# Attention's probabilities and values kept in plain float32, two heads side by side in TensorE's column halves

## The chip, the cores and the metric

The kernel runs on one core of one Trainium2 chip. The metric is the time of one execution in device microseconds (us); the median of three runs is shown.

## The reference

Two layers of a diffusion backbone over 1024 latent tokens and 256 context tokens of width 1024, all in float32. Each layer mixes tokens by attention, by a gated recurrence and by a Fourier transform, all reading one projection, and then applies a gated feed-forward network with a short convolution. What matters here is the attention: 8 query heads and 2 key/value heads of 64 channels.

```python
def attend(q, k, v):
    s = jnp.einsum('bhgqd,bhkd->bhgqk', q, k).astype(jnp.float32) * (HEAD_DIM ** -0.5)
    p = jax.nn.softmax(s, axis=-1).astype(v.dtype)
    return jnp.einsum('bhgqk,bhkd->bhgqd', p, v)
```

Latent tokens read 1280 keys (context and latent); context tokens read the 256 context keys, and only in the first layer.

## The kernel before

Tokens are cut into ten tiles of 128: two of context, eight of latent tokens. Attention (`attention`) works on **units**: one tile of queries and one pair of heads. Layer 0 has 40 units, 8 of them on context tiles; layer 1 has 32. For a unit, `score` multiplies queries by keys (L566, L567) in segments of at most 512 keys, takes the maximum (L569, L572) and the exponential (L576). `value` then multiplies probabilities by V. TensorE sums over the partition axis, so the probabilities must first be turned with the keys on partitions: a **step** takes two tiles of 128 keys and both heads, four transposes of 128x128 (L602), into one PSUM tile `ps_t` of which there are two. A latent unit has five steps, a context unit one: 64 x 5 + 8 = 328 steps.

The kernel's products of float32 numbers use the type `float32r` with operands split into a high part and the remainder. `ph` is the rounded copy of a step's turned probabilities (a cast on ScalarE, L607), `pl` what is left (a subtraction on VectorE, L608). V is stored as high, low, high (`use_kv`, L458 to L460), so that one product of `pl` with (low, high) and one of `ph` with (high, low), each with all 128 columns of the array and 256 moving columns (two heads side by side), add up the four partial products in the two halves of `ps_o`'s partitions. These are L612 and L614: four matmuls a step. At a unit's end the two halves of `ps_o` are added (`oa`, L619; `ob`, L620) and stored (L621). There is one `ps_o`.

`value` of one unit and `score` of the next are generators that alternate. Each step they `yield` a cost, and `interleave` lets the other work of the layer (late projections, then Fourier mixing, then the recurrence) run beside them in proportion; `LACE` has the shares. The order on an engine is fixed when the program is built: instructions are numbered in program order, `ahead(x)` subtracts the offset `AHEAD[layer][x]` from the number of those inside and leaves the counter where it was, and each engine takes the lowest number that is ready. Transposes ("pt") are pulled ahead by 50 in layer 0 and 30 in layer 1, score products ("qk") by 50 and 150; the products with V ("pv") and the split ("split") stay at their place. Beside these streams, on TensorE, run the projections (L158 to L160) and the recurrence's products (L773), which use parts of the array 64 rows by 32 or 64 columns; the products of the adaLN part (L246) use four column strips of 32.

Of the kernel before, what the change touches and what calls it, by code (L numbers as in the profile page):

```python
# [11 lines left out]
F32 = mybir.dt.float32  # L12
# [7 lines left out]
P = 128  # L20
# [5 lines left out]
NT = T // P  # L26
# [19 lines left out]
# how the parts of a layer's token mixing are laced, and which of their instructions go ahead of others  # L46
# [16 lines left out]
P_BUFS = {512: 10, 256: 5}  # L63

# [32 lines left out]
def hybrid_backbone_kernel(ctx: ExitStack, tc: tile.TileContext, A: dict, out: bass.AP):  # L97
# [50 lines left out]
    def w_stream(units, ahead=()):  # L148
        # weights split one unit ahead of the products that take them
        ahead = list(ahead) or [w_split(*units[0])]  # L150
        for n in range(len(units)):
            if n + len(ahead) < len(units) and len(ahead) < 2:
                ahead.append(w_split(*units[n + len(ahead)]))
            yield ahead.pop(0)
# [26 lines left out]
    def columns(pp, specs, eng=None):  # L181
        # parameter rows to one column per 128 of them
# [149 lines left out]
    # ================= token mixing: projections =================  # L332
# [15 lines left out]
    class Stages:  # L348
        # each use of a product runs its later stages after one and two further products
# [49 lines left out]
    def project_qkv(l, ww, hT, st, S, bg, tiles):  # L399
# [56 lines left out]
        def use_kv(i, acc):  # L456
            vv = acc[:, 128:256].rearrange("p (h c) -> p h c", h=2)
            nc.scalar.copy(V[:, i, :, 0, :], vv)  # L458
            nc.scalar.copy(V[:, i, :, 2, :], vv)
            nc.vector.tensor_tensor(out=V[:, i, :, 1, :], in0=vv, in1=f32(V[:, i, :, 0, :]), op=ALU.subtract)  # L460
# [75 lines left out]
    # ================= attention =================  # L536
    def attention(l, S, ap, psn, finished):
# [54 lines left out]
        def value(i, pr):  # L592
# [3 lines left out]
            o = psn.tile([P, 256], F32, tag="o", bufs=1, name="ps_o")  # L596
            for s2 in range(nk // 2):
# [5 lines left out]
                ph = ap.tile([P, 2, 256], F32R, tag="ph", bufs=2, name="ph")  # L603
                pl = ap.tile([P, 2, 256], F32R, tag="pl", bufs=2, name="pl")
                tv = t.rearrange("p s h n -> p s (h n)")
                with ahead("split"):
                    nc.scalar.copy(ph, tv)  # L607
                    nc.vector.tensor_tensor(out=pl, in0=tv, in1=f32(ph), op=ALU.subtract)  # L608
                with ahead("pv"):
                    for ss in range(2):  # L610
                        s = 2 * s2 + ss
                        nc.tensor.matmul(o, lhsT=V[:, s, kv, 1:3, :].rearrange("p a c -> p (a c)"), rhs=pl[:, ss, :],  # L612
                                         start=(s == 0), stop=False)
                        nc.tensor.matmul(o, lhsT=V[:, s, kv, 0:2, :].rearrange("p a c -> p (a c)"), rhs=ph[:, ss, :],  # L614
                                         start=False, stop=(s == nk - 1))
                yield 0.88
            oa = ap.tile([HD, 256], F32, tag="oa", bufs=1, name="oa")
            ob = ap.tile([HD, 256], F32, tag="ob", bufs=2, name="ob")
            nc.scalar.copy(oa, o[64:128, :])  # L619
            nc.vector.tensor_tensor(out=ob, in0=o[0:64, :], in1=oa, op=ALU.add)  # L620
            nc.sync.dma_start(  # L621
                out=S["mixA"][pr * P:(pr + 1) * P, i * P:(i + 1) * P].rearrange("(h v) n -> v h n", v=HD),
                in_=ob.rearrange("p (h n) -> p h n", h=2))
# [4 lines left out]
        for n, u in enumerate(units):  # L628
            gens = [value(*u)] + ([score(*units[n + 1])] if n + 1 < len(units) else [])
            lens = [keys(u[0]) // 2, 2]  # L630
# [28 lines left out]
    # ================= Fourier mixing =================  # L659
# [85 lines left out]
    # ================= gated linear recurrence =================  # L745
    def recurrence(l, S, gp2, gp, psum):
# [18 lines left out]
        def scores(keys, size, moving):  # L765
            # keys of each block of `size` tokens against as many queries; heads of the lower and of the
            # upper 64 channels go to different banks
# [36 lines left out]
        def pair_steps(i):  # L804
            # two tiles of tokens, 2 P of them, side by side
# [111 lines left out]
        # a pair of tiles starts when the one before is halfway  # L917
# [55 lines left out]
    # ================= residual update and layer norm =================  # L973
# [13 lines left out]
    def load_resid(pp, src, ga, ba, bufs=4, after=None, engs=None):  # L987
        r = pp.tile([P, D], F32, tag="r", bufs=bufs, name="r")
        if after is not None:
            # keeps the load, and what it sets off, behind the one that writes `after`  # L990
            nc.scalar.copy(r[:, 0:1], after)
# [32 lines left out]
    # ================= output projection =================  # L1024
# [35 lines left out]
    # ================= gated convolutional feed-forward =================  # L1060
# [24 lines left out]
    def ffn_weights(fp, n, nraw):  # L1085
        # every fourth unit in a place of its own: one more than the common ring holds
# [11 lines left out]
    def conv(l, j, part, o, u):  # L1098
        # u has one token more than o on either side
# [22 lines left out]
    # The up-projection of all latent tokens takes seven products of quarters in place of eight  # L1122
    # (Winograd's form of Strassen's identity). A: rows 1 value, 2 gate; columns 1 the lower, 2 the upper
    # channels. B: rows 1 the lower, 2 the upper channels; columns 1 the later, 2 the earlier tokens.
    #   S1 = A21 + A22   S2 = S1 - A11    S3 = A11 - A21   S4 = A12 - S2
    #   T1 = B12 - B11   T2 = B22 - T1    T3 = B22 - B12   T4 = T2 - B21
# [670 lines left out]
```

## Time and profile before

| | |
|---|---|
| median of 3 runs (lowest, highest) | 3447.15 us (3443.57, 3452.46) |
| profiled execution, first to last instruction (span) | 3438.2 us |
| TensorE (PE) busy | 3118.6 us, 91% |
| weight loads (PEld) busy | 2535.5 us, 74% |
| VectorE (DVE) busy | 2545.4 us, 74% |
| ScalarE (ACT) busy | 1547.9 us, 45% |
| GpSimd (POOL) busy | 1412.7 us, 41% |

The profiled execution is known by its span alone; the runs' times also hold what lies around it. Matmuls overlap each other: a matmul's listed duration is longer than the distance at which the next one can start. So the pace of TensorE is read from the starts, and its busy time as the time in which some matmul was under way.

### The profile page before, as it was taken

The page shows a single profiled execution, that of the slowest core. Times are in us where ns is not written, and L with a number is a line of the kernel's source. Part 1 is how long each engine was busy: PE and PEld are TensorE (multiplying, and loading weights), DVE is VectorE, ACT ScalarE, POOL GpSimd, SP SyncE. Part 2 cuts the span into 40 slices and gives each one's busy share as a digit, 9 for nine tenths or more (in the row PEclk, how much of TensorE's full clock was granted, in tenths as well). Part 3 has the DMA queues.
Part 4 walks back from the last instruction along what each step waited for, and adds up shares of the span by engine and source line. Part 5 has one row for each costly group of instructions (what it writes and reads, how often), then busy time and mean ns, then how long its engine had stood idle before and what let it go on. Part 6 is the DMA issues. An engine that isn't in the chain of part 4 may idle for free.

```text
span 3438.2 us, 55946 instructions
## 1 busy us (share of the span) xinstructions
PE 3118.6 (91%) x20897; PEld 2535.5 (74%) x20897; DVE 2545.4 (74%) x4167; ACT 1547.9 (45%) x3105; POOL 1412.7 (41%) x1138
## 2 busy tenths in 40 slices
PE   6999998989899999887899999998988889998885
PEld 4879976778666777666697888876766668776664
DVE  4614568877798887698766755668877798887888
ACT  4325556664443434333365435655642534444332
POOL 3521105422554444443435351115435645454545
PEclk9999999999999999999999999999989999999998
DMA  7643122127754443655675432122045532225643
GB/s 214 205 149 84 54 90 60 34 57 217 223 180 140 129 130 121 210 197 176 208 213 182 130 103 71 46 89 67 18 132 170 185 110 80 80 74 183 224 161 117
DMA packets 451396, 457.07 MB, mean 133 GB/s; under 512 B 31859, under 2 KB 343604, under 8 KB 451126
## 3 DMA queue, kind: packets, MB, share of 16 engines
q1 hardware_dynamic: 440342, 443.85, 40.9%
q0 software_dynamic: 10784, 9.66, 1.2%
q8 instruction: 165, 2.70, 0.3%
q14 instruction: 105, 0.86, 0.1%
HBM read 358.88 MB, written 94.54 MB: 132 GB/s over the span
## 4 chain that ended last, share of the span: by engine, by line
PE 17%; DVE 14%; issue 7%; POOL 6%; DMA 4%; ACT 2%; SPq 0%; POOLq 0%; DVEq 0%; ACTq 0%
POOL wlo L1216 3%; PE ps_t L602 2%; PE pu L159 2%; PE pu L158 2%; PE pu L160 2%; DVE cv L1105 1%; DVE wlo L1337 1%; PE ps_s L566 1%; DMA araw<-act 1%; PE ps_o L612 1%; PE ps_s L567 1%; PE ps_o L614 1%; PE pws L158 1%; PE pws L159 1%; PE pws L160 1%
## 5 line engine op out<-in xcount | busy, mean ns | idle before, releaser
L1216 POOL TENSOR_TENSOR wlo<-S,whi 128x512 fp32r<-128x512 f32 x176 | 282.5, 1615 | 279.3 <-ACT whi L1215 266.1
L1105 DVE SCALAR_TENSOR_TENSOR cv<-U,cw,cv 128x512 f32<-128x512 f32 x352 | 332.9, 994 | 32.5 <-ACT cv L1102 32.4
L158 PE MATMUL pd<-whi,wlo 128*128 128x512 f32 x616 | 251.4, 419 | 72.7 <-DVE wlo L1337 54.0
L569 DVE TENSOR_REDUCE mx<-ps_s 128x1 f32<-128x512 f32 (+1 forms) x400 | 222.2, 588 | 107.8 <-PE ps_s L567 106.5
L145 POOL TENSOR_TENSOR wlo<-raw,whi 128x1024 fp32r<-128x1024 f32 x69 | 167.4, 2429 | 300.6 <-ACT whi L144 300.6
L608 DVE TENSOR_TENSOR pl<-ps_t,ph 128x512 fp32r<-128x512 f32 x328 | 222.8, 685 | 85.2 <-ACT ph L607 83.0
L602 PE MATMUL ps_t<-ident,p 128*128 128x128 f32 x1312 | 261.9, 283 | 13.1 <-DVE pl L608 7.5
L159 PE MATMUL pd<-wlo,whi 128*128 128x512 f32 x616 | 255.6, 415 | 17.6 <-POOL wlo L1337 17.6
L576 ACT ACTIVATE p<-ps_s,mx 128x512 f32<-128x512 f32 (+1 forms) x400 | 242.7, 615 | 51.8 <-DVE mx L572 42.1
L607 ACT CAST ph<-ps_t 128x512 fp32r<-128x512 f32 x328 | 190.8, 589 | 160.8 <-PE ps_o L614 80.6
L160 PE MATMUL pd<-whi 128*128 128x512 f32 x616 | 252.0, 409 | 0.0
L1102 ACT ACTIVATE cv<-U,cb,cw 128x512 f32<-128x512 f32 x176 | 137.2, 812 | 254.3 <-DVE U L1231 209.6
L158 PE MATMUL pxs<-whi,hlo 128*128 128x256 f32 x752 | 221.6, 295 | 5.7 <-DVE hraw L1504 4.3
L1337 POOL TENSOR_TENSOR wlo<-raw,whi 128x1024 fp32r<-128x1024 f32 (+1 forms) x60 | 156.5, 2616 | 160.2 <-ACT whi L1336 151.0
L159 PE MATMUL pxs<-wlo,hhi 128*128 128x256 f32 x752 | 216.5, 288 | 0.5 <-DVE wlo L145 0.4
L160 PE MATMUL pxs<-whi,hhi 128*128 128x256 f32 x752 | 216.4, 288 | 0.0
L158 PEld LDWEIGHTS pd<-whi,wlo 128*128 128x128 f32 x616 | 122.0, 199 | 114.8 <-DVE wlo L1337 56.1
L612 PE MATMUL ps_o<-pl,V 128*128 128x256 f32 x656 | 200.4, 322 | 6.7 <-DVE pl L608 4.8
L1216 POOL TENSOR_TENSOR wlo<-raw,whi 128x512 fp32r<-128x512 f32 x108 | 149.9, 1395 | 128.0 <-ACT whi L1215 119.1
L556 POOL DMA_DIRECT2D qt<-QT x72 | 40.3, 560 | 373.9 <-PE ps_s L567 277.1
L602 PEld LDWEIGHTS ps_t<-ident,p 128*128 128x128 f32 x1312 | 164.2, 143 | 36.5 <-DVE pl L608 12.3
L1231 DVE TENSOR_TENSOR U<-pu,U 128x512 f32<-128x512 f32 x252 | 167.3, 685 | 25.5 <-PE pu L160 17.2
(395 smaller groups left out, 9680.2 us busy)
## 6 DMA issues: line engine op xcount, KB each, us to landing
raw<-in_w_up_dram SPq DMA_DIRECT2D x144, 512.0 KB
raw<-in_w_down_dram SPq DMA_DIRECT2D x102, 512.0 KB
raw<-in_w_ada_dram SPq DMA_DIRECT2D x96, 512.0 KB
araw<-act SPq DMA_DIRECT2D x80, 512.0 KB
act<-cv SPq DMA_DIRECT2D x88, 256.0 KB
raw<-in_w_in_dram SPq DMA_DIRECT2D x36, 512.0 KB
y<-r SPq DMA_DIRECT2D x28, 512.0 KB
r<-y SPq DMA_DIRECT2D x26, 512.0 KB
```

The source lines that it names most:

```text
L158: nc.tensor.matmul(o, lhsT=al, rhs=bh, start=start, stop=False)
L159: nc.tensor.matmul(o, lhsT=ah, rhs=bl, start=False, stop=False)
L160: nc.tensor.matmul(o, lhsT=ah, rhs=bh, start=False, stop=stop)
L569: nc.vector.tensor_reduce(out=mx[:, j:j + 1], in_=t[:, 0:n], axis=AX.X, op=ALU.max)
L576: nc.scalar.activation(out=t, in_=sc[j][:, 0:n], func=AF.Exp, bias=mx[:, 3:4], accum_out=su[:, h, j:j + 1])
L602: nc.tensor.transpose(t[:, ss, h, :], in_=ps2[h][2 * s2 + ss], identity=ident)
L607: nc.scalar.copy(ph, tv)
L608: nc.vector.tensor_tensor(out=pl, in0=tv, in1=f32(ph), op=ALU.subtract)
L612: nc.tensor.matmul(o, lhsT=V[:, s, kv, 1:3, :].rearrange("p a c -> p (a c)"), rhs=pl[:, ss, :], start=(s == 0), stop=False)
L1105: nc.vector.scalar_tensor_tensor(out=o, in0=u[:, tap:tap + n], scalar=convw[l][tap][:, c:c + 1], in1=o, op0=ALU.mult, op1=ALU.add)
L1216: nc.gpsimd.tensor_tensor(out=lo, in0=src, in1=f32(hi), op=ALU.subtract)
L1337: eng.tensor_tensor(out=lo, in0=src, in1=f32(hi), op=ALU.subtract)
```

## The change

The turned probabilities are copied once, in plain float32, to `tt` (eight buffers): steps 1 and 3 by VectorE, the others by ScalarE. V is stored once, in plain float32. The products of a unit are no longer made step by step: after its last step, one burst of 20 calls (4 for a context unit) multiplies V (128 keys by 64 channels) by 128 columns of one head; the first head's result goes to the lower 64 partitions of `ps_o`, the second head's to the upper 64, in turn. `ps_o` has 128 columns in place of 256 and holds finished sums, so `oa` and the addition go; `ob` is a copy. The costs that `value` yields sum to the same for a unit, half of it behind the burst, and its number of pieces in the alternation with `score` is one more. `AHEAD` and `LACE` stay as they are. Comments are removed throughout; the rest of the diff is this:

```diff
+TT_BUFS = 8
+TT_DVE = (1, 3)
...
         def use_kv(i, acc):
             vv = acc[:, 128:256].rearrange("p (h c) -> p h c", h=2)
-            nc.scalar.copy(V[:, i, :, 0, :], vv)
-            nc.scalar.copy(V[:, i, :, 2, :], vv)
-            nc.vector.tensor_tensor(out=V[:, i, :, 1, :], in0=vv, in1=f32(V[:, i, :, 0, :]), op=ALU.subtract)
+            nc.scalar.copy(V[:, i, :, :], vv)
...
-            o = psn.tile([P, 256], F32, tag="o", bufs=1, name="ps_o")
+            turned = []
             for s2 in range(nk // 2):
                 t = psn.tile([P, 2, 2, P], F32, tag="pt", bufs=2, name="ps_t")
                 with ahead("pt"):
                     for ss in range(2):
                         for h in range(2):
                             nc.tensor.transpose(t[:, ss, h, :], in_=ps2[h][2 * s2 + ss], identity=ident)
-                ph = ap.tile([P, 2, 256], F32R, tag="ph", bufs=2, name="ph")
-                pl = ap.tile([P, 2, 256], F32R, tag="pl", bufs=2, name="pl")
-                tv = t.rearrange("p s h n -> p s (h n)")
+                tt = ap.tile([P, 2, 2, P], F32, tag="tt", bufs=TT_BUFS, name="tt")
                 with ahead("split"):
-                    nc.scalar.copy(ph, tv)
-                    nc.vector.tensor_tensor(out=pl, in0=tv, in1=f32(ph), op=ALU.subtract)
-                with ahead("pv"):
-                    for ss in range(2):
-                        s = 2 * s2 + ss
-                        nc.tensor.matmul(o, lhsT=V[:, s, kv, 1:3, :].rearrange("p a c -> p (a c)"), rhs=pl[:, ss, :],
-                                         start=(s == 0), stop=False)
-                        nc.tensor.matmul(o, lhsT=V[:, s, kv, 0:2, :].rearrange("p a c -> p (a c)"), rhs=ph[:, ss, :],
-                                         start=False, stop=(s == nk - 1))
-                yield 0.88
-            oa = ap.tile([HD, 256], F32, tag="oa", bufs=1, name="oa")
-            ob = ap.tile([HD, 256], F32, tag="ob", bufs=2, name="ob")
-            nc.scalar.copy(oa, o[64:128, :])
-            nc.vector.tensor_tensor(out=ob, in0=o[0:64, :], in1=oa, op=ALU.add)
-            nc.sync.dma_start(
-                out=S["mixA"][pr * P:(pr + 1) * P, i * P:(i + 1) * P].rearrange("(h v) n -> v h n", v=HD),
-                in_=ob.rearrange("p (h n) -> p h n", h=2))
+                    if s2 in TT_DVE:
+                        nc.vector.tensor_copy(tt, t)
+                    else:
+                        nc.scalar.copy(tt, t)
+                turned.append(tt)
+                yield 0.44
+
+            o = psn.tile([P, P], F32, tag="o", bufs=1, name="ps_o")
+            with ahead("pv"):
+                for s in range(nk):
+                    for h in range(2):
+                        nc.tensor.matmul(o[64 * h:64 * h + 64, :], lhsT=V[:, s, kv, :], rhs=turned[s // 2][:, s % 2, h, :],
+                                         start=(s == 0), stop=(s == nk - 1))
+            ob = ap.tile([P, P], F32, tag="ob", bufs=2, name="ob")
+            nc.vector.tensor_copy(ob, o)
+            nc.sync.dma_start(out=S["mixA"][pr * P:(pr + 1) * P, i * P:(i + 1) * P], in_=ob)
+            yield 0.44 * (nk // 2)
...
-            lens = [keys(u[0]) // 2, 2]
+            lens = [keys(u[0]) // 2 + 1, 2]
...
-        S["V"] = kvp.tile([P, NT, 2, 3, HD], F32R, name="V")
+        S["V"] = kvp.tile([P, NT, 2, HD], F32, name="V")
```

## Rows read from the trace of the kernel before

**Rows 1.** Four stretches: start:end, length, busy PE, PEld, DVE, ACT, POOL, clock, DMA share, GB/s.
```profile
314.00:478.00 164.00, 161.47 (x1139) 145.52 (x1138) 95.65 (x214) 97.98 (x249) 21.93 (x21) 1.00 0.26 78
520.00:760.00 240.00, 217.55 (x3529) 178.33 (x3527) 193.35 (x478) 162.31 (x446) 101.64 (x136) 0.94 0.16 42
2095.00:2286.00 191.00, 189.40 (x1311) 165.96 (x1310) 126.27 (x264) 126.08 (x324) 23.93 (x24) 1.00 0.23 68
2305.00:2512.00 207.00, 187.25 (x2837) 148.18 (x2837) 168.58 (x395) 128.63 (x347) 89.40 (x117) 0.96 0.14 40
```
**Rows 2.** Groups by line, weight loads: busy, mean ns, idle before and its releasers.
```profile
L602 PEld LDWEIGHTS ps_t<-ident,p 128*128 128x128 f32 x1312 | 164.2, 143 | 36.5 <-DVE pl L608 12.3 <-issue 5.2 <-ACT p L576 3.3
L612 PEld LDWEIGHTS ps_o<-pl,V 128*128 128x128 f32 x656 | 126.4, 193 | 22.9 <-DVE pl L608 9.6 <-DVE ob L620 3.8 <-issue 2.2
L566 PEld LDWEIGHTS ps_s<-KT,qt 128*128 128x128 f32 x400 | 73.5, 192 | 33.5 <-ACT p L576 22.1 <-DMA qt<-QT 3.2
```

**Rows 3.** Groups by line: the split of the turned probabilities and a PSUM copy.
```profile
L608 DVE TENSOR_TENSOR pl<-ps_t,ph 128x512 fp32r<-128x512 f32 x328 | 222.8, 685 | 85.2 <-ACT ph L607 83.0
L607 ACT CAST ph<-ps_t 128x512 fp32r<-128x512 f32 x328 | 190.8, 589 | 160.8 <-PE ps_o L614 80.6 <-PE ps_t L602 71.2 <-DVE mx L572 2.0
L302 DVE COPY stT<-pT 128x512 f32<-128x512 f32 x28 | 19.1, 682 | 4.1 <-PE pT L294 4.1
```

**Rows 4.** Timeline of TensorE, 557.9 to 559.4 us (start, duration, instruction).
```profile
557.98 0.28 PE L612 MATMUL ps_o<-pl,V 128*128 128x256 f32 x1
558.10 0.28 PE L614 MATMUL ps_o<-ph,V 128*128 128x256 f32 x1
558.30 0.85 PE L773 MATMUL psc<-W 64*64 64x64 f32 x32
559.09 0.64 PE L602 MATMUL ps_t<-ident,p 128*128 128x128 f32 x2
```

**Rows 5.** Timeline of TensorE, 484.2 to 487 us: plain float32, 512 columns.
```profile
484.28 2.74 PE L728 MATMUL pq<-st,at 128*128 128x512 f32 x6
486.86 0.38 PE L602 MATMUL ps_t<-ident,p 128*128 128x128 f32 x2
```

**Rows 6.** Timeline of TensorE, 1202.0 to 1203.8 us, and the tile pada (min/median/max).
```profile
1202.16 0.40 PE L159 MATMUL pu<-T3l,whi 128*128 128x512 f32 x1
1202.40 0.39 PE L160 MATMUL pu<-T3h,whi 128*128 128x512 f32 x1
1202.72 0.64 PE L246 MATMUL pada<-raw,scol 128*32 128x256 f32 x8
1203.29 0.51 PE L158 MATMUL pu<-T4h,wlo 128*128 128x512 f32 x1
...
L246 PE MATMUL pada<-raw,scol x768: 379/403/637, 5.6 to 1394.4; 128*32 128x256 f32 x192
```

**Rows 7.** Groups by line, weight loads, 285 to 785 us.
```profile
L773 PEld LDWEIGHTS psc<-W 64*64 64x64 f32 x160 | 5.0, 149 | 3.0 <-issue 1.2 <-POOL W L875 1.0
```

**Rows 8.** Timeline of TensorE, 373.4 to 374.6 us.
```profile
373.51 0.37 PE L612 MATMUL ps_o<-pl,V 128*128 128x256 f32 x1
373.72 0.27 PE L602 MATMUL ps_t<-ident,p 128*128 128x128 f32 x1
373.74 0.36 PE L614 MATMUL ps_o<-ph,V 128*128 128x256 f32 x1
373.94 0.27 PE L602 MATMUL ps_t<-ident,p 128*128 128x128 f32 x1
```

**Rows 9.** Timeline of TensorE, 613.7 to 615.2 us.
```profile
613.77 0.33 PE L602 MATMUL ps_t<-ident,p 128*128 128x128 f32 x1
614.02 0.25 PE L773 MATMUL psc<-W,kc 64*32 64x32 f32 x2
614.20 0.33 PE L602 MATMUL ps_t<-ident,p 128*128 128x128 f32 x1
```

## The prediction

> **What bounds the kernel now.** I read the four stretches in which attention runs beside other work first [rows 1]: layer 0 beside the late projections (314 to 478 us) and beside the recurrence (520 to 760), then the same two of layer 1. Beside the projections TensorE is busy 161.5 of 164 us and 189.4 of 191; beside the recurrence 217.6 of 240 and 187.3 of 207. VectorE is at 58 to 81%, ScalarE at 60 to 68%. So in these 802 us TensorE sets the pace: it has 46 us of visible idle time, nearly all beside the recurrence, and work taken from VectorE and ScalarE is worth only the TensorE idle time that it caused.
>
> Next I read the groups by line for what that idle time waits on [rows 2]. The weight loads of the turning transposes (L602) and of the products (L612) waited 12.3 and 9.6 us for `pl` (the subtraction on VectorE that closes a step's split and frees its `ps_t` buffer), the product another 3.8 us for `ob`, which frees the single `ps_o`; the transposes waited 3.3 us and the score products (L566) 22.1 us for the exponentials on ScalarE. Together 51 us out of some 800: this is all that shorter queues can give back.
>
> **The change, part by part.** There are 72 pairs of heads ("units"): 64 with five steps of two key tiles, 8 with one step; 328 steps.
>
> *VectorE and ScalarE.* VectorE loses 328 subtractions of 0.685 us (223 us) and gains 128 copies (steps 1 and 3 of 64 units) at the 0.682 us of a copy of the same shape out of PSUM: 87 us, net 136 less. ScalarE loses 328 casts of 0.589 us and gains 200 copies of that price, net 75 less [rows 3]. `oa` and two instructions per tile of V go too. On the path to the end this counts only through the waits above: all of `pl` and `ob` (25.7 us) and, since the exponentials queue behind less, about half of the 25.4 us behind them: -38 us. Bounds: -15, if the copies simply take the place of `pl` as the releaser of `ps_t`, and -60, if the recurrence's VectorE steps also come sooner.
>
> *The products alone.* Before, a step's four products of 256 columns follow each other at 0.12 us [rows 4], so the 20 of a unit take 2.40 us. A plain float32 product runs as two passes: six passes of 512 columns take 484.28 to 486.86, 0.43 us each [rows 5], so a pass of 128 columns needs 0.107 us. Forty passes in two column halves are 20 rounds if the halves run together. That they can is in the trace twice: 32 matmuls of 64 columns on 64x64 tiles, 0.054 us each, end within 0.85 us [rows 4], half of what they would need one after another; and eight passes of 256 columns in four column strips, 0.215 us each, end within 0.64 us, where one by one they would need 1.7 [rows 6]. One of the eight lasts 0.38 us at least, so the last starts 0.26 after the first, and the second round of four begins at 0.24, not 0.215: 0.025 over for four tiles in turn. With two I take half of that, 0.12 us a round, 2.40 us a unit: no gain and no loss. Bounds 0.107 and 0.14 us a round: -16 to +26 us over 64 units.
>
> A rule speaks against this. The Trainium skill ("TensorE: Matmul & The Clock Gate", Part 3, The mechanism) says that a weight load overlaps running matmuls only where the row group differs, and column halves share it. The only 64-column load here lasts 0.149 us [rows 7]; with it exposed in each of 20 rounds the burst would be some 3 us longer, about +190 us in all. The trace bears it out poorly: in [rows 6] the four strips share their rows, and both rounds with eight loads still end in 0.64 us.
>
> *Going in and out.* From a full-width product to a tiled one the next start comes after 0.20 instead of 0.12 us [rows 4], and after 0.32 instead of 0.24 [rows 6]: +0.08. On the way out the last pass in [rows 6] starts at 1202.72 + 0.26 and streams for 0.215, to 1203.19; the next product starts at 1203.29: +0.10. Before, a unit's products switch nothing. 72 x 0.18 = +13 us.
>
> *Interruptions.* This is the term that decides. The order on TensorE is fixed when the program is built: every instruction gets the next number in program order, those under `ahead` get that number less an offset and leave the counter alone, and TensorE takes the lowest number that is ready. Where two streams share numbers they alternate one by one; 373.51 to 373.94 shows product, transpose, product, transpose [rows 8]. Today this costs nothing: transpose and product together take 0.23 us, 0.11 + 0.12. In a burst each alternation leaves the column mode and comes back. [Rows 9] price that: with single tiled products between transposes a cycle takes 0.43 us, 0.25 in and 0.18 out. Less the transpose (0.11) and two passes of 32 columns (0.05) that is 0.27, of which 0.03 is the second pass's weight load, hidden in a pass of 0.107. Besides, a call between two transposes has no partner: 0.215 instead of 0.12. So 0.24 + 0.10 = 0.34 us per interruption.
>
> How many? A burst takes 20 numbers, b to b+19; copy and store make 22. Then the other stream runs for 2.2 of the unit's 6.55 cost points. Beside the projections of layer 0 it has about 52 numbers a unit, so 17 follow on average (in lumps of 26), and the next unit's first transposes stand at b+39, less the offset of 50: b-11, ahead of the burst. But its steps 1 to 4 come within some 5 to 30 numbers more (b+3 to b+15, 16 transposes), and its score products, also pulled by 50, near b. They fall into the burst's own numbers; two `ps_t` buffers and eight `tt` buffers hold back only some. I take 6 interruptions a burst for the 15 units beside projections and Fourier. Beside layer 0's recurrence a unit is about 160 numbers long, 40 follow the burst, and the first step lands near b+12, the others beyond: 3 each for 17 units. In layer 1 the transposes are pulled by 30 alone and land at or behind the burst's end; score products are pulled by 150 and come whenever a `ps_s` buffer comes free: 1.2 each for 32 units. 90 + 51 + 38 = 179, x 0.34 = +61 us. Bounds: none (0), and ten in every burst (640 x 0.34 = +218).
>
> *The rest.* The store keeps its number and bytes on SyncE's queue. The loads of q on GpSimd keep their place. The smaller `ps_o` is now held for a burst, not for a whole unit; its wait is counted above. The new wait, of the first product of a burst for the last `tt`, has the burst and nothing else behind it on TensorE; the transposes are pulled 30 to 50 numbers ahead of it, so the copy is done: nothing. A copy that waits for one of the eight `tt` buffers holds up maxima on VectorE or exponentials on ScalarE behind it, but the buffer comes free after the burst's first four products: inside the bounds of the first term.
>
> **Sum:** 0 + 13 + 61 - 38 = +36 us. The profiled execution had 3438.2 us from its first to its last instruction, so 3474; the median run of 3447.15 lies 8.95 above that span, so 3483 for a run.
>
> **Rivals.**
> 1. *The bursts stay whole* (faster). If nothing enters them, the third term goes: 0 + 13 - 38 = -25, 3422; with the better bounds of products and waits 3384. For it: the 51 us of waits are real, and a product of the next unit enters only if its numbers and its buffers fit. Against it: in layer 0 the numbers coincide, and the alternation in [rows 8] is just that. It decides from below about one interruption a burst: 64 x 0.34 = 22 us leaves nothing over the waits.
> 2. *A draw.* A third to half of the interruptions, 25 us, eat what the waits give: 3447.
> 3. *The halves do not run together* (or their loads lie open, as the rule above has it). Forty passes of 0.107 are 4.3 us instead of 2.4: +122 over 64 units; with 13 for the switches, 179 x 0.24 = 43 for interruptions, which then break no pair, and -38: +140, 3587. Against it stand [rows 4] and [rows 6]; for it only that no row here has 128 rows by 64 columns.
> 4. *A large part of the gain is real but in the wrong place.* Beside the projections TensorE has 4 us of idle time in 355 us [rows 1]; if the relief lands there, it is worth nothing, and the first term shrinks to its bound of -15: 3506. This belongs to the forecast's upper side.
>
> **Numbers.** Forecast (with the fourth case) 0.50, its own range 3460 to 3530; whole bursts 0.28; draw 0.14; serial halves 0.08. Leaving out a tenth on either side gives 3412 to 3545. A measurement of this kernel tells about 0.3%, 10 us, from no change: faster by more 0.27, within 0.15, slower 0.58.
>
> **What would show it.** Burst alone: where 40 passes of `ps_o` follow each other, first to last start near 2.3 us; 4.2 would be serial halves. Switches: 0.25 us from a transpose to a product of the burst, about 0.2 back. Interruptions: in layer 0 beside the projections, transposes between single products of `ps_o`, six or so a unit, few in layer 1; so layer 0's attention should grow by more than layer 1's. Waits: none left for `pl` or `ob`, those of L566 for exponentials halved. VectorE should fall by about 150 us and ScalarE by about 100 without a matching fall of the span. I am wrong if bursts are contiguous in layer 0, or if a transpose in a burst costs less than 0.2 us.

## The result, and the profile after

The changed kernel takes 3550.35 us (median of 4 runs, 3545.81 to 3553.13) against 3445.36 us (4 runs) of the kernel before, run beside it: a ratio of 1.0304, with a 95% interval of 1.0289 to 1.0319. That is 105 us more, where 36 had been forecast; the time lies 20 us beyond the forecast's own range (3460 to 3530) and 5 beyond the wide one (3412 to 3545). The profiled span grew from 3438.2 to 3549.6 us.

The page's first part, and the four stretches in which attention runs beside other work (the columns are those of [rows 1]; the stretches are moved to where this kernel does the same work):

```profile
PE 3241.6 (91%) x22209; PEld 2552.6 (72%) x22209; DVE 2436.5 (69%) x3947; ACT 1453.1 (41%) x2885; POOL 1415.0 (40%) x1138
...
320.00:484.00 164.00, 164.00 (x1163) 128.88 (x1161) 55.73 (x125) 66.61 (x175) 19.90 (x17) 1.00 0.16 49
558.00:822.00 264.00, 241.07 (x3868) 176.92 (x3867) 172.61 (x430) 137.90 (x390) 102.86 (x136) 0.95 0.14 40
2160.00:2380.00 220.00, 219.86 (x1622) 169.81 (x1621) 98.79 (x220) 107.07 (x285) 23.75 (x24) 1.00 0.20 59
2405.00:2618.00 213.00, 198.31 (x3097) 145.81 (x3096) 148.20 (x350) 106.81 (x300) 87.80 (x112) 0.94 0.13 38
```

VectorE is busy 109 us less and ScalarE 95 us less than before; TensorE is busy 123 us more, and its idle time (span less busy) went from 320 to 308 us. So the loss is TensorE's own, and of what the two relieved engines gave, these 12 us of idle time are the most that shows. In the stretches beside projections TensorE has no idle time left to see: 164.00 of 164 us and 219.86 of 220, where [rows 1] had 161.47 of 164 and 189.40 of 191.

Where in the program it went is told by the turning transposes, which run from the first to the last unit of a layer. The view is that of one tile (count, least/median/greatest ns, first and last start); first the kernel before, layer 0 and layer 1, then after:

```profile
L602 PE MATMUL ps_t<-ident,p x672: 270/272/477, 289.8 to 756.2; 128*128 128x128 f32 x168
...
L602 PE MATMUL ps_t<-ident,p x640: 270/272/476, 2095.5 to 2519.7; 128*128 128x128 f32 x160
```
```profile
L602 PE MATMUL ps_t<-ident,p x672: 270/273/476, 290.0 to 810.2; 128*128 128x128 f32 x168
...
L602 PE MATMUL ps_t<-ident,p x640: 270/273/476, 2157.3 to 2618.9; 128*128 128x128 f32 x160
```

Layer 0's attention grew from 466.4 to 520.2 us, layer 1's from 424.2 to 461.6: +54 and +37 of the 111 us by which the profiled span grew. The other 20 us lie between and behind these stretches (8 and 12), and no run says what they are; two runs of the kernel before can differ by as much (3433.63 to 3458.81 us in one set of 19).

The groups by line that answer to [rows 2] and [rows 3] (busy, mean ns, then idle before and its releasers; L602 transposes, L616 products, L606 and L608 the copies, L619 the last copy):

```profile
L602 PEld LDWEIGHTS ps_t<-ident,p 128*128 128x128 f32 x1312 | 162.9, 142 | 67.1 <-issue 45.0 <-ACT tt L608 3.4 <-ACT p L576 2.4
L616 PEld LDWEIGHTS ps_o<-tt,V 128*64 128x64 f32 x2624 | 170.4, 138 | 68.4 <-issue 34.5 <-DVE tt L606 2.4 <-DVE ob L619 2.1
L566 PEld LDWEIGHTS ps_s<-KT,qt 128*128 128x128 f32 x400 | 74.7, 195 | 38.0 <-ACT p L576 15.8 <-issue 9.0 <-DMA qt<-QT 3.0
...
L606 DVE COPY tt<-ps_t 128x512 f32<-128x512 f32 x128 | 87.9, 687 | 97.4 <-PE ps_t L602 96.5
L608 ACT COPY tt<-ps_t 128x512 f32<-128x512 f32 x200 | 117.6, 588 | 229.6 <-PE ps_t L602 228.8
L619 DVE COPY ob<-ps_o 128x128 f32<-128x128 f32 x72 | 20.8, 288 | 55.0 <-PE ps_o L616 54.5
```

What the loss looks like stands in the word "issue": weight loads that waited for nothing that the profile shows. It was 5.2 and 2.2 us for these two lines in [rows 2] and is 45.0 and 34.5. The waits for `pl` are gone, as foreseen, and small ones for `tt` stand in their place.

Now the timelines. A whole burst, by itself, and one in layer 0 beside projections (start, duration, instruction; a call is two passes, so x2 is one call and x40 the whole unit):

```profile
2234.83 0.52 PE L567 MATMUL ps_s<-KT,qt 128*128 128x256 f32 x2
2235.28 2.40 PE L616 MATMUL ps_o<-tt,V 128*64 128x128 f32 x40
2237.61 0.33 PE L602 MATMUL ps_t<-ident,p 128*128 128x128 f32 x1
```
```profile
334.65 0.28 PE L162 MATMUL pxs<-whi,hhi 128*128 128x256 f32 x1
334.86 1.31 PE L616 MATMUL ps_o<-tt,V 128*64 128x128 f32 x18
336.09 0.33 PE L602 MATMUL ps_t<-ident,p 128*128 128x128 f32 x1
336.35 0.43 PE L616 MATMUL ps_o<-tt,V 128*64 128x128 f32 x2
336.71 0.33 PE L602 MATMUL ps_t<-ident,p 128*128 128x128 f32 x1
336.97 0.43 PE L616 MATMUL ps_o<-tt,V 128*64 128x128 f32 x2
337.34 0.44 PE L602 MATMUL ps_t<-ident,p 128*128 128x128 f32 x2
```

The first shows the halves running together: 40 passes from the first start to the last end in 2.40 us. The last pass lasts some 0.27, so the first and last starts are 2.13 us apart, 0.11 us a round. The second shows the interruption: from 336.09 to 336.71 one transpose and one call take 0.62 us. Before, a transpose and a product took 0.23 [rows 8]; +0.39 for each. Counted by the order of starts, the products stand on TensorE in 409 runs instead of 72, so they are interrupted 337 times; 308 of the runs hold an odd number of calls, and one call in them has no partner in the other half. Layer 1, for which few interruptions were expected, has 144 of the 337; transposes stand in 114 of these and score products in 34. One of its bursts beside the projections, cut by score products, and a part of another, cut by transposes:

```profile
2180.88 0.65 PE L616 MATMUL ps_o<-tt,V 128*64 128x128 f32 x6
2181.46 0.50 PE L566 MATMUL ps_s<-KT,qt 128*128 128x512 f32 x1
2181.80 0.40 PE L567 MATMUL ps_s<-KT,qt 128*128 128x512 f32 x1
2182.12 1.09 PE L616 MATMUL ps_o<-tt,V 128*64 128x128 f32 x16
2183.15 0.50 PE L566 MATMUL ps_s<-KT,qt 128*128 128x512 f32 x1
...
2184.04 1.30 PE L616 MATMUL ps_o<-tt,V 128*64 128x128 f32 x18
```
```profile
2302.99 0.65 PE L616 MATMUL ps_o<-tt,V 128*64 128x128 f32 x6
2303.57 0.33 PE L602 MATMUL ps_t<-ident,p 128*128 128x128 f32 x1
2303.83 0.43 PE L616 MATMUL ps_o<-tt,V 128*64 128x128 f32 x2
2304.20 0.33 PE L602 MATMUL ps_t<-ident,p 128*128 128x128 f32 x1
```

### The profile page after: what moved, and what is told of

The parts are those of the page before. It is cut to its first block, busy times and chain, and to the rows that moved or that the text cites. A ratio compares the mean times of both kernels' runs of the same rounds, so it can differ in the third digit from the quotient of the medians.

```text
span 3549.6 us, 57914 instructions
## 1 busy us (share of the span) xinstructions
PE 3241.6 (91%) x22209; PEld 2552.6 (72%) x22209; DVE 2436.5 (69%) x3947; ACT 1453.1 (41%) x2885; POOL 1415.0 (40%) x1138
## 5 line engine op out<-in xcount | busy, mean ns | idle before, releaser
L602 PE MATMUL ps_t<-ident,p 128*128 128x128 f32 x1312 | 290.6, 294 | 3.3 <-ACT p L576 1.8
L616 PE MATMUL ps_o<-tt,V 128*64 128x128 f32 x2624 | 271.4, 289 | 3.6 <-DVE tt L606 1.9
L616 PEld LDWEIGHTS ps_o<-tt,V 128*64 128x64 f32 x2624 | 170.4, 138 | 68.4 <-issue 34.5
L608 ACT COPY tt<-ps_t 128x512 f32<-128x512 f32 x200 | 117.6, 588 | 229.6 <-PE ps_t L602 228.8
L602 PEld LDWEIGHTS ps_t<-ident,p 128*128 128x128 f32 x1312 | 162.9, 142 | 67.1 <-issue 45.0
```

Source lines behind the costliest of these rows:

```text
L602: nc.tensor.transpose(t[:, ss, h, :], in_=ps2[h][2 * s2 + ss], identity=ident)
L616: nc.tensor.matmul(o[64 * h:64 * h + 64, :], lhsT=V[:, s, kv, :], rhs=turned[s // 2][:, s % 2, h, :], start=(s == 0), stop=(s == nk - 1))
```

## The experiments

Theory: the order on TensorE cuts the bursts, each cut costs a change of the array's division in and out, and the lighter load of VectorE and ScalarE is worth little. Rivals: the products themselves are slower; the halves run one after the other; the shorter queues are worth tens of microseconds and hide a still larger loss. Ratios are to the kernel before, run on the same chip; brackets hold 95% intervals.

**The bursts whole** (from the changed kernel). The calls are pulled far ahead, and the first call reads the copy made last, so that it waits for all of them and nothing comes between; 72 runs.

```diff
-..."pt": 50, "split": 0, "pv": 0, ...
+..."pt": 50, "split": 0, "pv": 300, ...
-..."pt": 30, "split": 0, "pv": 0, ...
+..."pt": 30, "split": 0, "pv": 300, ...
-                for s in range(nk):
+                for s in range(nk - 1, -1, -1):
...
-                                         start=(s == 0), stop=(s == nk - 1))
+                                         start=(s == nk - 1), stop=(s == 0))
```

> The changed kernel with its bursts kept whole: the products with V get a low number (ahead by 300) and each burst begins with the last step's keys, so that all its 20 calls become ready at once; the program then has 72 unbroken runs on TensorE in place of 409. Theory (each entry into and exit from the column halves costs about 0.29 us, each call left without its partner 0.11 us): 337 runs x 0.29 + 308 x 0.11 = 131 us less than the changed kernel, about 3420. Rival (the products come too late in a unit, or plain float32 passes are slow by themselves): no change, about 3550. Second rival (switches cost it, but the relief of VectorE and ScalarE is worth nothing): about 3455.

3465.16 us, 1.0054 [1.0033, 1.0074]: +19 us. Of the 105 us, 86 go with the 337 interruptions: 0.255 us each, if the whole bursts lose nothing by their own order (the clock, further down, speaks against that). What is left, products, 72 ways in and out and whatever the relief gives, adds up to +19, where the forecast without interruptions had -25. The weight loads of [rows 2] stand idle for as long as before, 41.7 and 16.9 us in place of 36.5 and 22.9; the copies are named where `pl` was:

```profile
L602 PEld LDWEIGHTS ps_t<-ident,p 128*128 128x128 f32 x1312 | 165.1, 145 | 41.7 <-ACT tt L608 8.7 <-issue 7.9 <-DVE tt L606 6.2
L616 PEld LDWEIGHTS ps_o<-tt,V 128*64 128x64 f32 x2624 | 151.5, 144 | 16.9 <-ACT tt L608 11.3 <-issue 1.1 <-ACT kc L835 0.9
```

**Only the relief** (from the kernel before). The low part of the probabilities is left out, and the product that took it takes the rounded copy `ph` once more: no subtraction, no wait for it, the copies divided between VectorE and ScalarE as in the change; the number and shape of the products stay.

```diff
-                pl = ap.tile([P, 2, 256], F32R, tag="pl", bufs=2, name="pl")
...
-                    nc.scalar.copy(ph, tv)
-                    nc.vector.tensor_tensor(out=pl, in0=tv, in1=f32(ph), op=ALU.subtract)
+                    if s2 in (1, 3):
+                        nc.vector.tensor_copy(ph, tv)
+                    else:
+                        nc.scalar.copy(ph, tv)
...
-..., rhs=pl[:, ss, :],
+..., rhs=ph[:, ss, :],
```

> The kernel before with the relief of VectorE and ScalarE alone: the subtraction is left out and the product that took the remainder takes the rounded copy again, so the low part of the probabilities is left out of the result; steps 1 and 3 are copied by VectorE, the others by ScalarE. TensorE's instructions are the same in number and size. Theory: the relief is worth the waits that it removes, 25 to 40 us, about 3410. Rival (TensorE is the bound and the waits only move): 3435 to 3450.

3454.71 us, 1.0019 [1.0003, 1.0035]: nothing gained. The same lines as in [rows 2], of this kernel (L613 is the first product):

```profile
L602 PEld LDWEIGHTS ps_t<-ident,p 128*128 128x128 f32 x1312 | 168.3, 144 | 34.9 <-ACT ph L609 7.7 <-DVE ph L607 6.4 <-ACT p L576 3.7
L613 PEld LDWEIGHTS ps_o<-ph,V 128*128 128x128 f32 x656 | 128.4, 196 | 22.9 <-DVE ph L607 5.8 <-ACT ph L609 3.6 <-DVE ob L621 3.4
```

The waits changed their names: 34.9 and 22.9 us of idle time, as 36.5 and 22.9 before. The copy that replaces the subtraction ends the same idle time.

**Relief and burst, at full width** (the same, with the products of a unit in one burst behind its last step, five `ph` buffers).

```diff
+                turned.append(ph)
+                yield 0.44
...
+            with ahead("pv"):
+                for s in range(nk):
+                    ph = turned[s // 2]
...
```

> As the relief alone (low part of the probabilities left out), and the products of a unit deferred into one burst as in the change, but at the full width of the array in float32r, with five buffers of turned probabilities. Theory (a burst is slow only because it changes the array's mode): within 10 us of the relief alone, whatever runs between its products. Rival (the deferral and the interruptions themselves cost): 80 to 110 us above the relief alone.

3436.68 us, 0.9969 [0.9955, 0.9983]: 11 us faster than the kernel before, 18 faster than the relief alone and some 114 faster than the change, though its products stand in 394 runs, nearly as many as the 409 of the change. So neither the burst nor the number of its cuts costs by itself; the cuts cost where the products divide the array otherwise than their neighbours. That a cut at full width is free altogether is argued from [rows 8], not shown: the kernel before has its products in 500 runs, and no full-width burst was kept whole. This is also the run in which relief shows: the idle time before the same loads (L617 is the first product) fell from 59.4 us together to 40.4.

```profile
L603 PEld LDWEIGHTS ps_t<-ident,p 128*128 128x128 f32 x1312 | 166.4, 143 | 30.8 <-ACT ph L610 6.7 <-DVE ph L608 3.1 <-issue 3.0
L617 PEld LDWEIGHTS ps_o<-ph,V 128*128 128x128 f32 x656 | 127.4, 194 | 9.6 <-DVE ob L624 5.0 <-DVE ph L608 1.5 <-issue 0.3
```

**One full-width float32 call for both heads** (from the changed kernel). V twice side by side, so that one call of 256 columns makes both heads' sums without column halves; half of the results are not used.

```diff
-                    for h in range(2):
-                        nc.tensor.matmul(o[64 * h:64 * h + 64, :], lhsT=V[:, s, kv, :], rhs=turned[s // 2][:, s % 2, h, :],
-                                         start=(s == 0), stop=(s == nk - 1))
+                    nc.tensor.matmul(o, lhsT=V[:, s, kv, :, :].rearrange("p a c -> p (a c)"), rhs=turned[s // 2][:, s % 2, :, :].rearrange("p h n -> p (h n)"),
+                                     start=(s == 0), stop=(s == nk - 1))
```

> The changed kernel with its products at the full width: V is stored twice side by side (128 columns) and one plain float32 matmul takes both heads (256 moving columns), in the same bursts without protection; the program has 286 runs of them on TensorE. Theory: no mode changes, but each pair of key tiles costs two passes of 0.215 us in place of 0.235 together: 656 x 0.195 = 128 us over the kernel before, less 25 to 40 of relief: 3530 to 3545. Rival (an interruption of a plain float32 burst costs whatever its width): 286 x 0.3 more, about 3620.

3550.43 us, 1.0306 [1.0278, 1.0334]: the same time as the change, by another way. Its whole burst:

```profile
2201.83 4.48 PE L616 MATMUL ps_o<-tt,V 128*128 128x256 f32 x20
```

4.48 us instead of 2.40, 133 us over 64 units, and no change of division: since the times are equal, the column halves save some 130 us of product time against this form and lose about as much at their edges. Against the full-width burst above it is 114 us more, not even the whole 133; so its 286 runs leave no price for a cut of plain float32 as such.

**Four calls a step, no burst** (from the changed kernel, calls pulled by 300): 288 whole runs, 248 of four calls and 40 of eight.

```diff
-                turned.append(tt)
-                yield 0.44
+                with ahead("pv"):
+                    for ss in range(2):
+                        s = 2 * s2 + ss
+                        for h in range(2):
+                            nc.tensor.matmul(o[64 * h:64 * h + 64, :], lhsT=V[:, s, kv, :], rhs=tt[:, ss, h, :],
+                                             start=(s == 0), stop=(s == nk - 1))
+                yield 0.88
```

> The changed kernel without the burst: four calls in the column halves right after each step's copy, each group kept whole (ahead by 300); 288 unbroken runs on TensorE, none with an odd number of calls, in place of the 72 of the whole bursts. Theory (a clean entry and exit cost about 0.29 us): 216 x 0.29 = 63 us above the whole bursts, about 3528. Rival (what whole bursts lose comes from their late place in a unit, not from switches): at or below the whole bursts, 3440 to 3465.

3523.56 us, 1.0226 [1.0196, 1.0257]. Against the whole bursts 58.4 us for 216 more runs: 0.27 us for a clean way in and out, with whatever else their other place in the unit is worth. By that price the 72 of the whole bursts cost 19 us, which is all that they lose; products, waits and the granted clock together then come to nothing.

**The heads in turn** (the whole bursts, with all calls of one head before those of the other).

```diff
-                for s in range(nk - 1, -1, -1):
-                    for h in range(2):
+                for h in range(2):
+                    for s in range(nk - 1, -1, -1):
```

> The whole bursts with one loop turned round: all ten calls of the first head, then all ten of the second, instead of the heads in turn. Theory (halves run together only if neighbouring calls go to different halves): a burst takes 40 passes of 0.11 us one after another in place of 20, 64 x 2.2 = 137 us above the whole bursts, about 3602. Rival (the order of calls does not matter to the overlap): 3465.

3568.36 us, 1.0354 [1.0318, 1.0390], 103 us over the whole bursts. One burst:

```profile
2244.01 4.20 PE L616 MATMUL ps_o<-tt,V 128*64 128x128 f32 x40
```

4.20 us instead of 2.40: in one half the passes follow each other at about 0.10, in two halves in turn at 0.11 for two. Only the order of the calls was changed, so it is the alternation that makes the halves overlap.

**Transposes at their own place** (from the changed kernel).

```diff
-..."pt": 50, ...
+..."pt": 0, ...
-..."pt": 30, ...
+..."pt": 0, ...
-                    with ahead("qk" if (i, pr) != units[0] else "pt"):
+                    with ahead("qk"):
```

> The changed kernel with one number altered: the transposes are no longer pulled ahead (offset 0 in place of 50 and 30), so the next unit's transposes keep their place behind the burst; the program has 181 runs of products in place of 409, 108 of them with an odd number of calls in place of 308. Theory (the pulled transposes cut the bursts): with 0.29 us a run and 0.11 us an odd run, 43 us above the whole bursts, about 3508, some 42 us below the changed kernel. Rival (transposes at their place come too late for their copies, and TensorE waits): no gain over the changed kernel, 3550 or more.

3437.50 us, 0.9976 [0.9957, 0.9994]. The expectation was too high by 70 us. 181 runs are left, and 228 fewer at 0.255 are 58 us of the 113 gained. The other 55 may in part be the transposes themselves: they now stand in 279 groups instead of 756, and go over to or come from the recurrence's tiled products 99 times instead of 262. What that is worth no run separates; in the kernel before, the same edit takes 17 us off TensorE's busy time (below).

**Products one step later** (from the kernel before: three buffers each of `ph` and `pl`, nine of the probabilities' long segments instead of ten, the products of a step issued behind the next step's split).

```diff
+                if held:
+                    products(*held)
+                held = (s2, ph, pl)
                 yield 0.88
+            products(*held)
```

> The kernel before with the products of each step put behind the next step's turning (three buffers of each half of the split, nine of the probabilities' long segments), at the full width with the exact split. Theory (part of what the full-width burst gained, 18 us against the relief alone, comes from products that never wait for their split): 5 to 15 us below the kernel before. Rival (it came from the unit's order as a whole, or from fewer interruptions): no change, 3440 to 3455.

3454.87 us, 1.0024 [1.0008, 1.0040]: a miss. The waits were moved rather than taken away. The products (L602 here) wait 2.0 us for `pl` instead of 9.6, but 8.4 for `ob` instead of 3.8, and the transposes (L613 here) stand idle for 36.5 us as before:

```profile
L613 PEld LDWEIGHTS ps_t<-ident,p 128*128 128x128 f32 x1312 | 165.3, 143 | 36.5 <-DVE pl L619 9.6 <-issue 7.6 <-ACT p L576 2.1
L602 PEld LDWEIGHTS ps_o<-pl,V 128*128 128x128 f32 x656 | 126.4, 193 | 18.4 <-DVE ob L628 8.4 <-issue 2.0 <-DVE pl L619 2.0
```

**The offset of the transposes in the kernel before.** The edit of "Transposes at their own place", made in the kernel before.

> The kernel before with one number altered: the transposes are not pulled ahead (offset 0 in place of 50 and 30). It separates what pulled transposes cost other streams from what they cost the bursts. Theory (of the 113 us that this number was worth in the changed kernel, 83 came from the cut bursts and some 28 from transposes that cut the recurrence's tiled products and the projections): 20 to 30 us below the kernel before, about 3420. Rival (in the full-width kernel a transpose between other products costs nothing, and without the pull the products wait for their split): 3445 or more.

3439.76 us, 0.9985 [0.9973, 0.9997]: 5 us. So the 113 us of that edit in the changed kernel belong to it together with the column halves. Here it gives and takes: TensorE was busy for 3101.4 us of its span of 3439.0, 17 us less than before, but idle for 18 more. The products' weight loads (columns as in [rows 2]) now wait for `pl`, 55.0 us instead of 9.6:

```profile
L612 PEld LDWEIGHTS ps_o<-pl,V 128*128 128x128 f32 x656 | 125.4, 191 | 66.7 <-DVE pl L608 55.0 <-DVE mx L572 1.8 <-DVE ob L620 1.4
```

**Whole bursts and transposes at their place** (both edits in the changed kernel).

> The whole bursts (72 runs) and the transposes at their place together. Theory (both remove cuts, and cuts are all that the change costs): the 109 runs and 108 odd runs that the transposes at their place still leave are worth 0.27 and 0.11 us each, so 41 us below that kernel, about 3397. Rival (a burst forced whole loses as much by pushing all other work back, as the whole bursts' 28 us above the full-width burst suggest): 3430 to 3445.

3449.56 us, 1.0008 [0.9995, 1.0021]: no better with 72 runs than the 3437.50 with 181. To force a burst whole seems to have a price. One candidate is the granted clock. Beside the recurrences of the whole-burst kernel (columns as in [rows 1]):

```profile
526.00:796.00 270.00, 236.17 (x3904) 189.65 (x3905) 184.15 (x455) 143.70 (x400) 109.80 (x142) 0.89 0.19 56
2319.00:2545.00 226.00, 199.63 (x3203) 157.86 (x3202) 154.85 (x373) 113.44 (x315) 88.44 (x116) 0.89 0.14 42
```

0.89 is the mean of 2.4 GHz and stretches at 1.2; it was 0.95 and 0.94 in the change and 0.94 and 0.96 in [rows 1]. Summed over the clock's records, TensorE was at 1.2 GHz for 330 us in the whole bursts, 327 in this kernel, 263 with transposes at their place alone and 260 before. What in the order makes it fall was not tried, and that it is the cause of the lost time is argued, not shown. The runs allow an estimate: over the 77 runs of the kernel before, beside which the experiments ran, the time falls by about 2.0 us for each 0.001 of mean granted clock (3456.32 us at 0.957, 3435.35 at 0.964), and the mean of the whole bursts' runs is 0.953 against 0.960. That would be 15 of their 19 us. It would also be the 12 us between this kernel (0.956) and the one with the transposes alone at their place (0.962). No run sets the clock by itself. The change as it was given has 0.960, as the kernel before, so the clock is no part of its 105 us.

**All offsets of attention's matmuls at 0** (from the changed kernel): as "Transposes at their own place", and the score products too.

```diff
-    {"qk": 50, ... "pt": 50, ...
-    {"qk": 150, ... "pt": 30, ...
+    {"qk": 0, ... "pt": 0, ...
+    {"qk": 0, ... "pt": 0, ...
```

> The changed kernel with transposes and score products both at their place (offset 0 for both in both layers): 122 runs of products, 42 of them odd, nothing forced. Theory (cuts alone): 59 x 0.27 + 66 x 0.11 = 23 us below the kernel with the transposes alone at their place, about 3414. Rival (score products at their place make the exponentials late): 3440 to 3480.

3404.81 us, 0.9878 [0.9859, 0.9897]: 42 us faster than the kernel before, 146 faster than the change as it was given, and 33 below the transposes alone at their place, where 23 were expected. 122 runs are left, 42 of them odd.

**The same offsets in the kernel before.**

> The kernel before (full-width products, split probabilities) with the offsets of transposes and of score products at 0 in both layers: the same edit that brought the column halves from 3550 to 3405 us. My theory: its products switch no mode, so order alone is worth little here, as the transposes' offset alone was worth 5 us: 3425 to 3445 us. Then some 30 us of the 40 by which the column halves beat the kernel before with these offsets belong to the change itself. Rival: the order alone does it, whatever the products: 3395 to 3415 us, and the column halves pay nothing.

3459.0 us, 1.0032 [1.0020, 1.0044]: 11 us slower than before, above both expected ranges, and 54 us slower than the column halves with the same offsets. The page's first part and the products of both; first the kernel before with offsets 0 (span 3459.8), then the column halves (span 3400.2):

```profile
PE 3090.1 (89%) x20897; PEld 2529.8 (73%) x20897; DVE 2549.2 (74%) x4167; ACT 1543.4 (45%) x3105; POOL 1411.0 (41%) x1138
...
L612 PE MATMUL ps_o<-pl,V 128*128 128x256 f32 x656 | 200.6, 327 | 57.4 <-DVE pl L608 34.4
...
L612 PEld LDWEIGHTS ps_o<-pl,V 128*128 128x128 f32 x656 | 127.6, 195 | 88.9 <-DVE pl L608 63.3
```
```profile
PE 3082.6 (91%) x22209; PEld 2510.5 (74%) x22209; DVE 2427.3 (71%) x3947; ACT 1445.9 (43%) x2885; POOL 1415.0 (42%) x1138
...
L602 PE MATMUL ps_t<-ident,p 128*128 128x128 f32 x1312 | 201.8, 281 | 9.3 <-DVE tt L606 6.1
...
L616 PE MATMUL ps_o<-tt,V 128*64 128x128 f32 x2624 | 177.6, 280 | 3.1 <-DVE tt L606 1.7
L602 PEld LDWEIGHTS ps_t<-ident,p 128*128 128x128 f32 x1312 | 150.0, 143 | 36.2 <-DVE tt L606 11.1
```

This says what the offsets were for. With them at 0 TensorE is busy less in both (3090.1 and 3082.6 us against 3118.6), with the transposes no longer strewn among other matmuls (366 and 285 groups of them; 690 in the kernel before, 756 in the change). In the full-width kernel the products then stand right behind their own split, wait for `pl` for 63.3 us at the weight load, and TensorE's idle time goes from 320 to 370 us. The burst comes a unit's work later and needs only a copy: its idle time stays at 318. So the lead of the transposes hid the split in the old kernel; in the new one there is nothing left for it to hide, and the same lead puts the next unit's transposes into the burst.

## Why the prediction was wrong

The direction was right and so was the mechanism of the loss: bursts cut by the order of the numbers, each cut paid in changes of the array's division. The gain set against it did not come, and the sizes were off:

| step | forecast us | measured us | from |
|---|---|---|---|
| products alone, with the waits given back | 0 and -38 | about 0 together | whole bursts (+19) less 72 x 0.27 |
| ways in and out | 72 x 0.18 = 13 | 72 x 0.27 = 19 | four calls a step |
| interruptions | 179 x 0.34 = 61 | 337 x 0.255 = 86 | change less whole bursts |
| sum | 36 | 105 | |

The first row is what is left over, and the rows share one unknown: what the whole bursts lose by their own order. If that is the 15 us estimated from the clock, the first row is -15 and the third 101, 0.30 for each cut; the sum stays. Of the 69 us between forecast and result, 38 are the first row, 25 the interruptions and 6 the ways in and out.

*The step that failed most* is the first: "all of `pl` and `ob` (25.7 us) and [...] about half of the 25.4 us behind them: -38 us." The waits for `pl` went, the idle time did not: before the weight loads of transposes and products it was 59.4 us, and it is 58.6 in the whole bursts, with the copies to `tt` named in its place. That the copies would take the place of `pl` had been the bound of -15; they did, and relief alone gave +6 us instead of -38, a step's lag +8. The most that any such run gave is 11 us, for the full-width burst, where this idle time did fall. A wait of 12.3 us that ends last by `pl` is no gain of 12.3 us where the copy that follows frees the same buffer at nearly the same time. The fourth rival, relief in the wrong place, was on the forecast's side and had the right sign, but was given 23 us and not 38.

*The count* failed in layer 1. The prediction had there that "the transposes are pulled by 30 alone and land at or behind the burst's end", and counted score products alone, "1.2 each for 32 units"; the trace has 144 cuts, 4.5 each. The score products came as forecast: they stand in 34, 1.1 each, as at 2181.46. It is the transposes that land inside the burst, as at 2303.57: they stand in 114, and in 78 of the 88 that fall ahead of the recurrence. In layer 0 the estimate was 141; it was 193: 99 in the 15 units beside the projections and the Fourier mixing, 6.6 each instead of six; 87 in 17 beside the recurrence, five instead of three; and 7 in the units on context tiles, which had been given none.

*The price* of 0.34 lies between what the runs give. The difference of times divided by cuts is 0.255, the cycle of single calls in the trace 0.39. The two need not agree: a quarter of the runs hold an even number of calls, 34 cuts hold the recurrence's tiled products, and the whole bursts, which are the base of the first figure, seem to pay for their order themselves; how much was not separated. That 61 is as near to 86 as it is was in part luck: at a price of 0.34 the 337 cuts would have made 115. It was right that a transpose in a burst costs more than 0.2 us.

*The products* were right: 0.11 us a round against 0.12 taken, and the rival of serial halves fell by the 2.40 us of a whole burst, against 4.20 with the heads in turn; that its 3587 us lies nearer to the result than the forecast is accident. The rule that stood against it, that a weight load overlaps running matmuls only where the row group differs (the Trainium skill, "TensorE: Matmul & The Clock Gate", Part 3, The mechanism), does not hold here as the prediction read it; the same section excepts loads into the background weight buffer, which no run here can tell apart. The halves share all rows, and yet a call in the one runs with a call in the other; even in one half, passes follow at 0.10 us beside loads of 0.140 us.

*Going out* to a full-width product was put at 0.10 over the usual distance and *in* at 0.08; the runs give 0.27 for both together. The rows they came from had four strips and a long streaming product as the neighbour. That is 6 of the 69 us.

*Of what was to show*, these came: a burst by itself with 2.13 us from first to last start (2.3 was said), transposes between single products, no waits for `pl`, layer 0 growing by more than layer 1. The last came more weakly than the counts of the prediction had it: by 54 to 37 us, at 193 to 144 cuts instead of 141 to 38. Two came short: the waits of L566 for exponentials went from 22.1 to 15.8 us, not to half, and VectorE fell by 109 us instead of about 150.

## What to carry to other kernels

A change of the operands' form can be right and its order wrong: offsets tuned for one chain of waits (transposes ahead to hide a split) can be the very thing that harms the next, so such offsets belong to the change and are tried with it; here that was worth 146 us. Before a matmul is put into part of the array, count its runs between other forms, not only its passes. And a wait in the profile is worth its length only if nothing else ends a moment later: remove it alone first, as the relief here, and look whether the idle time goes with it.

## What the runs showed of the hardware

A clean way into column halves and out again costs 0.27 us (216 of them, 58.4 us, by the difference of two runs); a single plain float32 call of two passes between two transposes makes a cycle of 0.62 us, against 0.23 for a full-width product of 256 columns in the same place. Two column halves run fully beside each other if the calls alternate, and not at all if they come one half after the other (2.40 and 4.20 us for 40 passes of 128 columns). A full-width burst in 394 runs took 3436.68 us, some 114 less than the column halves in 409. The mean granted clock beside the recurrence was 0.89 when bursts were forced whole, against 0.95 and 0.94 in the change, and 0.953 against 0.960 over whole runs; its cause stays open.
